# A trunk with mixture-of-experts layer, one core: heavy and light experts in turn instead of four heavy ones and then four light ones

## The chip, the cores and the metric

The program runs on one core of a Trainium2 chip. The metric is the device time of one execution in microseconds (us), 1356.88 us as the median of 3 runs of the kernel before (1356.76 to 1357.43).

The engines are TensorE (PE in the tables; PEld is its loading of the stationary operand), VectorE (DVE), ScalarE (ACT), GpSimd (POOL) and SyncE (SP), which here issues nearly all loads.

## The reference, cut to what matters

Two layers on 256 tokens of width 1024, all in float32. Each layer has a block of four token mixers and a feed-forward part. That of layer 0 is dense. That of layer 1, about half of the time, is a mixture of 8 experts of which each token takes two:

```
def swiglu(t, w1, w3, w2):
    return (jax.nn.silu(t @ w1) * (t @ w3)) @ w2

def moe_swiglu(h, router, w1, w3, w2):
    logits = (t @ router);  top_vals, top_idx = lax.top_k(logits, 2)
    weights = jax.nn.softmax(top_vals, axis=-1)
    combine = sum(one_hot(top_idx, 8) * weights)            # (256, 8)
    out = combine[:, 0:1] * swiglu(t, w1[0], w3[0], w2[0])
    for e in range(1, 8):
        out = out + combine[:, e:e+1] * swiglu(t, w1[e], w3[e], w2[e])
```

w1 and w3 of an expert are 1024 x 2816, w2 is 2816 x 1024; the three are 34.6 MB, those of eight experts 277 MB. A final RMSNorm follows.

## The kernel before

**Products in pieces.** A float32 weight tile is split into a part `hi` (ACT, a copy to fp32r, L145) and a rest `lo` (DVE, raw minus hi, L165); activations are split in the same way. A product is then `prod` (L579): hi by hi, activation lo by weight hi, activation hi by weight lo, three matmuls for each block of 128 rows.

**Tiles and homes.** All weights come in tiles of 128 x 2048 floats (1 MB, in transfers 1024.0 KB). `WeightStream` (L65) holds a plan, which is the list of all tiles in the order of their use. A tile is loaded by SP into a "raw" home, split into a "hi" home and a "lo" home, and multiplied. `SLOTS` (L40) names the homes of each phase of the program by letters; a letter can be raw in one phase and hi or lo in another. `take` picks a home whose last owner is done. A load can be issued when the lo split of the raw home's last owner is done, a hi split when PE is done with the hi home's last owner, and a lo split likewise. How many raw homes a phase has is so how far loads can run ahead of PE.

**An expert** has six chunks of columns, `CHUNKS`: five of 512 and one of 256. The program goes in steps (expert, chunk): the tiles of w1 and w3 of a step (two each, one each for the short chunk), then the w2 tiles of the step before (two, or one). An expert has 33 tiles' worth of weights.

**Heavy and light.** The experts are sorted on the chip by their number of tokens, expert 0 first whatever its number. SP reads the sorted order into registers (L1197) and loads the weights of an expert by register. The first four places (`e < LIGHT`) are heavy: 128 token slots, `prod` with three products, ACT's silu (L1231), DVE's product (L1232), four transposes on PE (L1357), split into `ah` and `al`. The last four are light: up to 64 tokens each, hi and lo of the tokens side by side as 128 columns, so `both` (L586) needs two products, one with the weight's hi and one with its lo. The two halves are then added by matmuls with a folded identity (L1440), and silu, product and splitting are done on 64 columns.

**Around them.** `gather` (L1246) picks the tokens of a group of experts from the normed tokens `th`, `tl` by matmuls with 0/1 matrices `picks`: group 0 is places 0 and 1, group 1 places 2 and 3, group 2 places 4 to 7. After each pair of places `scatter` adds their outputs to x: 16 matmuls (L1595) and four additions on DVE (L1604); places 6 and 7 are added singly. `place` and `weigh` make the matrix and the weights for that, once for each pair (5th step of the even place).

**Order.** In steps 1 to 23 (heavy) the order of the instructions is found by a scheduler at build time. From step 24 on, `light` writes it out by hand: with each tile `i` of the plan PE's matmuls come first, then ACT's hi split of tile i+4, then DVE's lo split of tile i+2 (`AHEAD_HI`, `AHEAD_LO`), with a list `todo` of what else goes on each engine behind which tile. Engines work in this order.

**Routing** is ahead of that, while PE multiplies the first chunk of expert 0 for all tokens (`dense`, banks `da` and `db`). DVE finds the two best experts of each token, casts the choice to bf16 (`selb`, L1057), and PE counts positions by matmuls with it (`posps`, L1061) between the `dense` matmuls.

Of the kernel before, what the change touches and what calls it, by code (L numbers as in the profile page):

```python
# [18 lines left out]
P = 128  # L19
D = 1024  # L20
# [24 lines left out]
    "moe0": {"raw": "ABCDHLstuwxyz", "hi": "EFG", "lo": "IJK"},  # L45
    "moe1": {"raw": "ABCDHLstux", "hi": "EFG", "lo": "IJK"},
    "moe2": {"raw": "ABCDHLstu", "hi": "EFG", "lo": "IJK"},
    "moe3": {"raw": "ABCDstu", "hi": "EFGH", "lo": "IJKL"},
    "moe4": {"raw": "ABCDstuyz", "hi": "EFGH", "lo": "IJKL"},
    "moe5": {"raw": "ABCDstyz", "hi": "EFGH", "lo": "IJKL"},  # L50
    "end": {"raw": "ABCDstyz", "hi": "EFGH", "lo": "IJKL"},
# [6 lines left out]
M0, M1, ML, MQ, M2, END = 6, 11, 24, 27, 40, 47  # L58
# [12 lines left out]
class WeightStream:  # L71
# [6 lines left out]
    def __init__(self, tc, plan, slots):  # L78
        self.tc, self.nc, self.plan, self.slots = tc, tc.nc, plan, slots
        self.gate = []  # L80
        self.pools, self.owner = {}, {}
# [8 lines left out]
    def open(self, pool, names):  # L90
        for name in names:
            self.pools[name] = pool

    def take(self, kind, j, dt):
# [13 lines left out]
        return self.pools[slot].tile([P, 2048], dt, tag=slot, name=slot)  # L108
# [123 lines left out]
class Trunk:  # L232
# [758 lines left out]
    def setup_moe(self, l):  # L991
# [14 lines left out]
        self.fold = self.const.tile([P, Q], F32, name="fold")  # L1006
# [83 lines left out]
    def rank(self, mp, rp, cnt, pos):  # L1090
# [10 lines left out]
        number = self.slots[:, :NE]  # L1101
        to = rp.tile(pairs, F32, name="to")
        nc.vector.tensor_tensor(
            to, rank[:, None, :].to_broadcast(pairs), number[:, :, None].to_broadcast(pairs), op=ALU.is_equal
# [59 lines left out]
    def moe(self, l, next_gain):  # L1164
# [5 lines left out]
        with self.pool("moe") as mp:  # L1170
            self.line_up(mp, 320)
# [39 lines left out]
            self.overflow(l, th, tl, cw, pos, cnti)  # L1211

    def picks(self, ep, pos, group):


        shape, e0 = ([P, 2, 1, P], 2 * group) if group < 2 else ([P, 4, 2, Q], LIGHT)
        n, size = shape[1], shape[3]
        out = []
        for t in range(NT):
            room = ep.tile([P, 2 * T], F32R, tag=f"pick{t}", name=f"pick{t}")  # L1220
            pick = room[:, : n * shape[2] * size].rearrange("p (e d s) -> p e d s", e=n, d=shape[2])
            self.nc.vector.tensor_tensor(
                pick, self.slots[:, None, None, :size].to_broadcast(shape),
                pos[:, t, e0 : e0 + n, None, None].to_broadcast(shape), op=ALU.is_equal,
# [15 lines left out]
    def experts(self, l, ep, ap, xp, tok, cw, pos, pick, g0):  # L1240
# [5 lines left out]
        def gather(group, part, bank=self.mm):  # L1246
            if part == 0:
                if group == 1:
                    xe[1] = tuple(self.extra.tile([P, NK, 2, P], F32R, tag=n, name="xe" + n) for n in "yz")
                else:  # L1250
                    room = xp.tile([P, 2 * 2048], F32R, tag="xe", name="xe")
                    if group == 0:
                        xe[0] = tuple(
                            room[:, j * 2048 : (j + 1) * 2048].rearrange("p (k e s) -> p k e s", k=NK, e=2) for j in range(2)
                        )
                    else:
                        x4 = room.rearrange("p (k e s) -> p k e s", k=NK, e=4)
                        xe[2] = x4[:, :, :, :Q], x4[:, :, :, Q:]
                        xe["both"] = x4
            ps = bank("gps")  # L1260
            d0 = 2 * part
            n = xe[group][0].shape[2]
            for d in range(2):
                self.pick_cols(
                    ps[:, d * T : (d + 1) * T].rearrange("p (e s) -> p e s", e=n), tok,
                    slice((d0 + d) * P, (d0 + d + 1) * P), pick,
                )
            self.hilo(*(x[:, d0 : d0 + 2] for x in xe[group]), ps.rearrange("p (d e s) -> p d e s", d=2, e=n))

        for part in range(4):  # L1270
            gather(0, part, self.acc)
# [3 lines left out]
        def first_act():  # L1275

            act = act_pair()
            for f0 in range(0, 4, 2):
                ps = self.mm("g0ps")
                for f in range(2):  # L1280
                    self.pick_cols(ps[:, f * T : (f + 1) * T].rearrange("p (e s) -> p e s", e=2), g0, slice((f0 + f) * P, (f0 + f + 1) * P), pick)
# [3 lines left out]
        steps = [(e, c) for e in range(NE) for c in range(len(CHUNKS))]  # L1285
        acts, ys, done = {0: first_act()}, {}, []
        wsl = ep.tile([P, NE], F32, name="wsl")

        def mask(t, pair, j):
            return pick[t][:, 2 * pair + j - (LIGHT if pair >= 2 else 2 * pair)].rearrange("p d s -> p (d s)")  # L1290
# [37 lines left out]
        for s in range(1, ML):  # L1328
# [3 lines left out]
            xv = xe[e // 2]  # L1332
            outs = []
            for nm in ("w1", "w3"):
                ps = self.mm(nm)
                nt = NK // nk
                for k0 in range(nt):
                    w = ws.get((nm, l, e, c, k0))
                    self.prod(
                        ps[:, :n], lambda i, k: xv[i][:, k0 * nk + k, e % 2, :], lambda j, k: w[j][:, k, :],  # L1340
# [4 lines left out]
            if len(done) == 2:  # L1345
                self.scatter(done, put)
                done = []
            if s % 12 == PLACE:
                put = place(s // 12)
                weigh(s // 12)  # L1350
            y = self.expert_down(l, ep, *steps[s - 1], acts.pop(s - 1), ys, wsl)
            if y is not None:
                done.append((steps[s - 1][0], y))
            nf = n // P
            ps = self.mm("actps")
            for f in range(nf):
                nc.tensor.transpose(ps[:, f * P : (f + 1) * P], g[:, f * P : (f + 1) * P], self.ident)  # L1357
            act = act_pair()
            self.hilo(*(x[:, :nf, :] for x in act), ps[:, :n].rearrange("p (f s) -> p f s", f=nf))
            acts[s] = act  # L1360
            if e in (1, 3) and c < 4:
                if c == 0:
                    pick = self.picks(ep, pos, e // 2 + 1)
                gather(e // 2 + 1, c)
# [11 lines left out]

        ws.release()
# [4 lines left out]
    def light(self, l, ep, ap, x4, acts, ys, done, wsl, masks, place_parts):  # L1382
# [3 lines left out]
        bank, half, now = {}, {}, [0]  # L1386
# [11 lines left out]
        def up(i, w, nm, e, c, k0):  # L1398
            c0, n = CHUNKS[c]
            nk, s = 2048 // n, e * len(CHUNKS) + c  # L1400
            if k0 == 0:
# [3 lines left out]
            self.both(  # L1405
                ps[:, :n], lambda k: x4[:, k0 * nk + k, e - LIGHT, :], lambda j, k: w[j][:, k, :],
                range(nk), start=k0 == 0, stop=last,
            )
            if nm == "w1" and k0 == 0:
                if s % 12 == PLACE:  # L1410
# [14 lines left out]

            def copy():
# [6 lines left out]
            nf, box = n // P, {}  # L1433
# [100 lines left out]
    def down_part(self, e, ps, act, k0, rhs, start, stop):  # L1534
        if e < LIGHT:
# [4 lines left out]
    def expert_down(self, l, ep, e, c, act, ys, wsl):  # L1540
# [4 lines left out]
        c0, n = CHUNKS[c]  # L1545
        for k0 in range(n // 256):
            w = ws.get(("w2", l, e, c, k0))
            for half in range(2):
                self.down_part(
                    e, y[half], act, k0, lambda j, k: w[j][:, k, half * 512 : (half + 1) * 512],  # L1550
                    c == 0 and k0 == 0, c == len(CHUNKS) - 1 and k0 == n // 256 - 1,
# [203 lines left out]
```

## Time and profile before

| | |
|---|---|
| device time, median of 3 | 1356.88 us |
| profiled execution, own time | 1354.36 us |
| its span | 1352.7 us |
| PE / PEld busy | 1308.0 / 1154.1 us |
| DVE / ACT / POOL busy | 1055.1 / 871.5 / 29.2 us |
| HBM read | 384.99 MB, 285 GB/s over the span |

The page's row of 40 slices shows DMA at 110 to 370 GB/s in the first three quarters and at 407 to 412 GB/s in the last quarter, without a break until the last slice. The mixture is in the second half: the first step of expert 0 begins at 595 us, place 1 at 709.4 us, place 4 (the first light one) at 1002 us, and the last matmuls are at 1339 us. A busy time of PE is a union of modelled, overlapping spans; a time between two instructions of one kind is the better measure of its pace.

### The profile page before, as it was taken

What the parts mean: (1) busy time and instruction counts of PE and PEld (TensorE: products, weight loads), DVE (VectorE), ACT (ScalarE), POOL (GpSimd) and SP (SyncE); (2) the same over time, 40 slices, a digit from 0 to 9 for tenths busy, and PEclk for the clock granted to TensorE, in tenths of its full rate; (3) what the DMA queues carried; (4) which work ended last, traced back from release to release, by engine and by line L of the source; (5) the groups of instructions that cost most, each with busy time, mean ns of one, the idle gap of its engine ahead of it and who ended that gap; (6) DMA issues with size and microseconds to landing.
All of it is one profiled execution on the core that took longest, in us unless ns stands there. A gap on an engine that the chain in (4) does not pass through costs nothing. (4 is left out here: it accounts for less than half of the span.)

```text
span 1352.7 us, 20123 instructions
## 1 busy us (share of the span) xinstructions
PE 1308.0 (97%) x8088; PEld 1154.1 (85%) x8088; DVE 1055.1 (78%) x874; ACT 871.5 (64%) x775; POOL 29.2 (2%) x52
## 2 busy tenths in 40 slices
PE   7999999999999999999999999999999989999995
PEld 7999999999989999978888888888887877777774
DVE  6976666444457856668988888988899989899996
ACT  5644445344437354556777777777788988888884
POOL 3110000000000000000000000000000000000000
PEclk9999999999999999999999999999999989999998
DMA  9736655555546395647989999999899999999992
GB/s 290 245 128 216 197 192 193 196 183 190 191 144 227 125 342 189 196 170 265 368 291 350 352 325 327 378 366 351 332 336 407 408 412 409 410 411 409 411 409 111
DMA packets 212128, 387.40 MB, mean 286 GB/s; under 512 B 7791, under 2 KB 98733, under 8 KB 212030
## 3 DMA queue, kind: packets, MB, share of 16 engines
q1 hardware_dynamic: 211214, 383.90, 78.6%
q0 software_dynamic: 816, 2.17, 0.6%
q8 instruction: 65, 1.06, 0.3%
q14 instruction: 33, 0.27, 0.0%
HBM read 384.99 MB, written 1.05 MB: 285 GB/s over the span
## 5 line engine op out<-in xcount | busy, mean ns | idle before, releaser
L165 DVE TENSOR_TENSOR J<-B,F 128x2048 fp32r<-128x2048 f32 (+1 forms) x33 | 72.2, 2189 | 36.6 <-ACT F L145 35.4
L145 ACT ACTIVATE F<-B 128x2048 fp32r<-128x2048 f32 (+1 forms) x33 | 60.6, 1838 | 41.0 <-PE mm L584 14.8
L165 DVE TENSOR_TENSOR L<-D,H 128x2048 fp32r<-128x2048 f32 (+1 forms) x29 | 64.1, 2213 | 24.3 <-ACT H L145 24.3
L165 DVE TENSOR_TENSOR I<-A,E 128x2048 fp32r<-128x2048 f32 (+1 forms) x27 | 59.7, 2210 | 27.2 <-ACT E L145 27.1
L871 ACT ACTIVATE sg<-mm,cols 128x256 f32<-128x256 f32 x64 | 26.8, 470 | 77.8 <-PE mm L584 49.7
L145 ACT ACTIVATE E<-A 128x2048 fp32r<-128x2048 f32 (+1 forms) x27 | 50.0, 1851 | 36.1 <-issue 12.6
L145 ACT ACTIVATE H<-D 128x2048 fp32r<-128x2048 f32 (+1 forms) x29 | 53.8, 1857 | 28.6 <-PE mm L584 11.0
L165 DVE TENSOR_TENSOR K<-C,G 128x2048 fp32r<-128x2048 f32 x24 | 55.0, 2290 | 16.8 <-ACT G L145 16.7
L145 ACT ACTIVATE G<-C 128x2048 fp32r<-128x2048 f32 x24 | 45.9, 1914 | 25.6 <-issue 11.7
L1440 PEld LDWEIGHTS actps<-fold,half 128*128 128x128 f32 x352 | 43.0, 191 | 2.2
L877 DVE TENSOR_TENSOR sg<-pr,sg 128x512 f32<-128x512 f32 x24 | 16.6, 692 | 33.2 <-ACT sg L871 33.2
L165 DVE TENSOR_TENSOR I<-s,E 128x2048 fp32r<-128x2048 f32 (+1 forms) x19 | 41.2, 2173 | 1.5 <-ACT E L145 1.3
L1440 PE MATMUL actps<-fold,half 128*128 128x64 f32 x352 | 41.9, 271 | 0.0
L145 ACT ACTIVATE E<-s 128x2048 fp32r<-128x2048 f32 (+1 forms) x19 | 34.6, 1827 | 9.3 <-PE w L584 5.5
L482 POOL TENSOR_TENSOR rstd<-rstd,mhalf 128x1 f32<-128x1 f32 (+1 forms) x14 | 12.5, 895 | 1284.1 <-ACT fo L487 744.0
L584 PE MATMUL w<-E,xe 128*128 128x512 f32 (+1 forms) x168 | 38.9, 372 | 0.0
L584 PE MATMUL mm<-hThi,F 128*128 128x256 f32 x256 | 35.9, 281 | 0.0
L584 PE MATMUL mm<-hThi,J 128*128 128x256 f32 x256 | 35.3, 279 | 0.0
L584 PE MATMUL mm<-hTlo,F 128*128 128x256 f32 x256 | 34.9, 278 | 0.0
L584 PE MATMUL mm<-hThi,G 128*128 128x256 f32 x240 | 33.8, 281 | 0.0
L584 PE MATMUL mm<-hTlo,G 128*128 128x256 f32 x240 | 33.6, 280 | 0.0
L584 PE MATMUL mm<-hThi,H 128*128 128x256 f32 x240 | 33.6, 280 | 0.0
(586 smaller groups left out, 3937.4 us busy)
## 6 DMA issues: line engine op xcount, KB each, us to landing
B<-in_moe_w_dram SPq DMA_DIRECT2D x29, 1024.0 KB, 5.6
C<-in_moe_w_dram SPq DMA_DIRECT2D x29, 1024.0 KB, 6.5
D<-in_moe_w_dram SPq DMA_DIRECT2D x29, 1024.0 KB, 9.5
s<-in_moe_w_dram SPq DMA_DIRECT2D x29, 1024.0 KB, 7.1
A<-in_moe_w_dram SPq DMA_DIRECT2D x28, 1024.0 KB, 10.8
t<-in_moe_w_dram SPq DMA_DIRECT2D x28, 1024.0 KB, 10.4
u<-in_moe_w_dram SPq DMA_DIRECT2D x24, 1024.0 KB, 8.1
y<-in_moe_w_dram SPq DMA_DIRECT2D x17, 1024.0 KB, 13.0
```

What stands on the lines that cost most here:

```text
L145: self.nc.scalar.activation(t[:, s], self.raw[j][:, s], AF.Copy)
L165: self.nc.vector.tensor_tensor(t[:, s], self.raw[j][:, s], self.hi[j][:, s].bitcast(F32), op=ALU.subtract)
L482: self.power = nc.gpsimd.tensor_tensor(r, t, self.mhalf[:, :n], op=ALU.pow)
L584: nc.tensor.matmul(ps, lhs(i, k), rhs(j, k), start=start and n == 0, stop=stop and n == len(steps) - 1)
L871: nc.scalar.activation(sg[:, s], psg[:, s], AF.Sigmoid, bias=self.col(l, "b_gate", i * 8 + 2 * j + c))
L877: nc.vector.tensor_tensor(sg, pr[j], sg, op=ALU.mult)
L1440: nc.tensor.matmul(out[:, o : o + Q], x[:, f * P : (f + 1) * P], self.fold, start=True, stop=True)
```

## The change

The order of the experts' places is now heavy, light, heavy, light, and so on: `RANK_AT` says which rank stands at which place. Groups to be gathered are places 0 and 2, "light" (1, 3, 5, 7), and places 4 and 6. Only the six steps of place 0 are left to the scheduler, and the seven other places are written out by hand in `rest`, which has got a branch for heavy places. The light tokens are gathered in steps 2 to 5 of place 0 (they were in place 3), the second heavy group in steps 18 to 21, in place 3. Picks have two sets of tiles.

The homes: the hi homes of the mixture are EFGH throughout (EFG for steps 1 to 23 before), the lo homes IJK throughout (IJKL from step 24 before). Raw homes are 12, 10, 9, 8, 10, 9, 9 in the phases that begin at steps 1, 2, 6, 11, 24, 40 and 47 (13 from step 1, 10 from 6, 9 from 11, 7 from 24, 9 from 27, 8 from 40 before). From step 24 on the tiles of `th` and `tl` are two of these homes (p and q, in rooms of 2048 + 128 floats). So that they can be reused, POOL writes the two tiles of normed tokens to DRAM (512.0 KB each) just after routing, for a branch (`overflow`) that runs only when an expert has more tokens than slots.

```
-    "moe0": {"raw": "ABCDHLstuwxyz", "hi": "EFG", "lo": "IJK"},
...
-    "moe3": {"raw": "ABCDstu", "hi": "EFGH", "lo": "IJKL"},
-    "moe4": {"raw": "ABCDstuyz", "hi": "EFGH", "lo": "IJKL"},
...
+    "moe0": {"raw": "ABCDLstuwxyz", "hi": "EFGH", "lo": "IJK"},
...
+    "moe3": {"raw": "ABCDLstu", "hi": "EFGH", "lo": "IJK"},
+    "moe4": {"raw": "ABCDLstupq", "hi": "EFGH", "lo": "IJK"},
...
-PHASES = ((1, "late"), (M0, "moe0"), (M1, "moe1"), (ML, "moe2"), (MQ, "moe3"), (M2, "moe4"), (END, "moe5"), (99, "end"))
+PHASES = ((1, "late"), (2, "moe0"), (6, "moe1"), (11, "moe2"), (24, "moe3"), (M2, "moe4"), (47, "moe5"), (99, "end"))
+RANK_AT = (0, 4, 1, 5, 2, 6, 3, 7)
+GATHER = 18
...
+                        for t in range(NT):
+                            nc.gpsimd.dma_start(self.a["normed"][t], self.htok[t])
...
+        ws.open(self.ypool, "pq", [(n, 2048 + 128) for n in ("yhi", "ylo")])
         ws.release()
         with self.tc.manual_schedule(engines={ACT, DVE, PE}):
-            self.light(l, ep, ap, xe["both"], acts, ys, done, wsl, masks, place_parts)
+            self.rest(l, ep, ap, xe, acts, act_pair, ys, wsl, masks, place_parts, gather_parts)
...
+            light = e % 2 == 1
+            if light:
+                x = xe["light"][e // 4]
+                self.both(
...
+            else:
+                x = xe[e // 4]
+                self.prod(
...
+            if not light:
+                if nm == "w1":
...
+                    at("hi", i + 4, silu)
+                    return
...
+                at("lo", i + 3, mult)
+                at("mm", i + 2, turn)
+                at("hi", i + 6, act_hi)
+                at("lo", i + 5, act_lo)
+                return
...
-        if e < LIGHT:
+        if e % 2 == 0:
             self.prod(ps, lambda i, k: act[i][:, 2 * k0 + k, :], rhs, range(2), start=start, stop=stop)
```

Of the instructions' order two places matter. The first is on PE, where a heavy and a light expert meet. Before, there is one such place, where step 23 ends and step 24 begins (`w` are the sums of w1 and w3, `yps` those of w2, `xe` the gathered tokens, E to H hi homes and I to L lo homes):

```order
L584 MATMUL yps<-I,ah 128x512 x4
L1357 MATMUL actps<-ident,g 128x128 x2
L590 MATMUL w_9497<-H,xe 128x512 x4
L590 MATMUL w_9497<-L,xe 128x512 x4
L590 MATMUL w_9497<-F,xe 128x512 x4
L590 MATMUL w_9497<-J,xe 128x512 x4
L590 MATMUL w_9524<-G,xe 128x512 x4
L590 MATMUL w_9524<-K,xe 128x512 x4
L590 MATMUL w_9524<-E,xe 128x512 x4
L590 MATMUL w_9524<-I,xe 128x512 x4
```

Now such places stand at every sixth step; this one is from light place 1 to heavy place 2:

```order
L594 MATMUL yps<-I,act 128x512 x2
L1527 MATMUL actps<-fold,half 128x64 x4
L588 MATMUL w_7915<-E,xe 128x512 x8
L588 MATMUL w_7915<-J,xe 128x512 x4
L588 MATMUL w_7915<-F,xe 128x512 x8
L588 MATMUL w_7915<-K,xe 128x512 x4
L588 MATMUL w_7957<-G,xe 128x512 x8
L588 MATMUL w_7957<-I,xe 128x512 x4
L588 MATMUL w_7957<-H,xe 128x512 x8
L588 MATMUL w_7957<-J,xe 128x512 x4
```

A tile takes eight matmuls in a light expert and twelve in a heavy one; the change alternates stretches of 33 tiles of the two kinds.

The second place is on DVE, in the routing ahead of the experts. Before (`selb` is what PE's position matmuls wait for; I, J are lo homes, y, z raw ones):

```order
L1025 TENSOR_REDUCE top_k<-top_m 128x2
L1026 TENSOR_TENSOR top_m<-top_m,top_k 128x16
L1055 TENSOR_TENSOR sel<-top_m 128x16
L1057 CAST selb<-sel 128x16
L165 TENSOR_TENSOR I<-y,E 128x2048
L1067 SCALAR_TENSOR_TENSOR pos<-posps,sel 128x16
L1070 TENSOR_SCALAR pos<-pos 128x16
L1096 SCALAR_TENSOR_TENSOR key<-posps,first_key 128x8
L165 TENSOR_TENSOR J<-z,F 128x2048
```

And now:

```order
L1032 TENSOR_REDUCE top_k<-top_m 128x2
L169 TENSOR_TENSOR I<-y,H 128x2048
L1033 TENSOR_TENSOR top_m<-top_m,top_k 128x16
L1062 TENSOR_TENSOR sel<-top_m 128x16
L169 TENSOR_TENSOR J<-z,E 128x2048
L1064 CAST selb<-sel 128x16
L1074 SCALAR_TENSOR_TENSOR pos<-posps,sel 128x16
```

Two lo splits have moved ahead of the cast. On PE nothing has moved there: the position matmuls still stand behind the `db<-J` matmuls of the second token tile and ahead of the `db<-G` ones.

## Rows read from the trace of the kernel before

**Rows 1.** Windows: busy us (instructions) of PE, PEld, DVE, ACT, POOL; clock; DMA; GB/s.

```profile
1002.00:1082.35 80.35, 78.30 (x398) 64.28 (x397) 77.73 (x51) 71.87 (x60) 0.00 (x0) 1.00 1.04 409
1082.35:1167.10 84.75, 77.79 (x370) 62.59 (x369) 79.21 (x48) 72.16 (x60) 0.00 (x0) 0.94 1.05 410
1167.10:1250.70 83.60, 78.89 (x394) 63.27 (x393) 79.30 (x53) 71.83 (x61) 0.00 (x0) 1.00 1.05 410
1250.70:1337.40 86.70, 80.61 (x388) 62.49 (x387) 80.71 (x62) 70.71 (x69) 0.00 (x0) 1.00 0.90 353
709.40:1002.00 292.60, 292.60 (x1417) 244.93 (x1416) 258.97 (x158) 215.66 (x152) 0.00 (x0) 1.00 0.94 344
```

**Rows 2.** Timeline of PE, light steps: start, us, what; a fold ends a step.

```profile
1057.27 1.89 PE L1440 MATMUL actps<-fold,half 128*128 128x64 f32 x16
1071.14 1.89 PE L1440 MATMUL actps<-fold,half 128*128 128x64 f32 x16
...
1081.35 1.00 PE L1440 MATMUL actps<-fold,half 128*128 128x64 f32 x8
...
1166.11 1.00 PE L1440 MATMUL actps<-fold,half 128*128 128x64 f32 x8
...
1249.68 1.00 PE L1440 MATMUL actps<-fold,half 128*128 128x64 f32 x8
...
1323.00 1.90 PE L1440 MATMUL actps<-fold,half 128*128 128x64 f32 x16
...
1337.41 2.45 PE L1578 MATMUL scps<-y,put 128*128 128x512 f32 x8
```

**Rows 3.** Timeline of DVE, inside a light step.

```profile
1128.25 2.28 DVE L165 TENSOR_TENSOR L<-D,H 128x2048 fp32r<-128x2048 f32 x1
1130.45 0.42 DVE L1457 TENSOR_TENSOR act<-gf,act 128x256 fp32r<-128x256 f32 x1
1130.79 2.28 DVE L165 TENSOR_TENSOR J<-y,F 128x2048 fp32r<-128x2048 f32 x1
```

**Rows 4.** Timeline of PE, heavy steps; the transposes end a step.

```profile
840.91 0.60 PE L1357 MATMUL actps<-ident,g 128*128 128x128 f32 x4
...
858.91 0.60 PE L1357 MATMUL actps<-ident,g 128*128 128x128 f32 x4
875.85 0.60 PE L1357 MATMUL actps<-ident,g 128*128 128x128 f32 x4
...
936.35 0.60 PE L1357 MATMUL actps<-ident,g 128*128 128x128 f32 x4
954.20 0.60 PE L1357 MATMUL actps<-ident,g 128*128 128x128 f32 x4
```

**Rows 5.** DVE's groups in place 4: the additions of a scatter.

```profile
L1604 DVE TENSOR_TENSOR x<-x,scps 128x512 f32<-128x512 f32 x4 | 2.6, 678 | 0.0
```

**Rows 6.** Timeline of PE in the routing.

```profile
613.84 1.08 PE L584 MATMUL da<-I,hThi 128*128 128x512 f32 x4
...
616.58 1.08 PE L584 MATMUL db<-J,hThi 128*128 128x512 f32 x4
617.51 0.18 PE L1061 MATMUL posps<-selb,before 128*128 128x8 bf16 x1
```

**Rows 7.** Timeline of DVE in the routing.

```profile
614.49 0.18 DVE L1055 TENSOR_TENSOR sel<-top_m 128x16 f32<-128x16 f32 x1
614.70 0.17 DVE L1057 CAST selb<-sel 128x16 bf16<-128x16 f32 x1
```

**Rows 8.** Timeline of ACT in the routing.

```profile
622.57 1.92 ACT L145 ACTIVATE G<-C 128x2048 fp32r<-128x2048 f32 x1 [3.82 <-DVE sort L1110]
```

**Rows 9.** DMA issues: queue, times, size, us from issue to landing.

```profile
gain<-in_norm_ffn_dram POOLq DMA_DIRECT2D x2, 512.0 KB, 6.4
B<-in_moe_w_dram SPq DMA_DIRECT2D x29, 1024.0 KB, 5.6
```

**Rows 10.** Waits in places 4 to 7: total, times, longest.

```profile
PE yps L590 <- DVE act L1457: 3.6, 2, 2.0
```

More of the change, by code (lines that the diff above doesn't have):

```diff
@@ L107, in take @@
         self.owner[slot] = (kind, j)
[L108 removed]
+        tag, size = self.tags[slot]
+        return self.pools[slot].tile([P, size], dt, tag=tag, name=slot)[:, :2048]
     def pair_due(self, slot, j):
@@ L1210, in moe @@
                     self.experts(l, ep, ap, xp, (th, tl), scw, spos, pick, (gh, gl))
-            self.overflow(l, th, tl, cw, pos, cnti)
+            self.overflow(l, cw, pos, cnti)
     def picks(self, ep, pos, group):
-        shape, e0 = ([P, 2, 1, P], 2 * group) if group < 2 else ([P, 4, 2, Q], LIGHT)
+        if group == "light":
+            shape, part = [P, 4, 2, Q], slice(1, NE, 2)
+        else:
+            shape, part = [P, 2, 1, P], slice(4 * group, 4 * group + 3, 2)
         n, size = shape[1], shape[3]
@@ L1244, in experts, with room, gather_sums @@
         xe = {}
[L1246 to L1259, printed above, removed]
+        def room(group):
+            if group == "light":
+                xe[group] = [self.extra.tile([P, NK, 2, P], F32R, tag=n, name="xe" + n) for n in "yz"]
+            else:
+                x = xp.tile([P, 2 * 2048], F32R, tag="xe", name="xe")
+                xe[group] = tuple(
+                    x[:, j * 2048 : (j + 1) * 2048].rearrange("p (k e s) -> p k e s", k=NK, e=2) for j in range(2)
+                )
+        def gather_sums(group, part, bank):
             ps = bank("gps")
-            d0 = 2 * part
-            n = xe[group][0].shape[2]
+            n = 4 if group == "light" else 2
             for d in range(2):
@@ L1326, in set_weights @@
             )
-        for s in range(1, ML):
+        for s in range(1, len(CHUNKS)):
             e, c = steps[s]
@@ L1344, in experts @@
             g = self.gate(ep, *outs, n)
[L1345 to L1364, printed above, removed]
+            if s == PLACE:
+                put = place(0)
+                weigh(0)
+            self.expert_down(l, *steps[s - 1], acts.pop(s - 1), ys)
+            acts[s] = self.turned(act_pair(), g, n // P)
+            if s >= 2:
+                if s == 2:
+                    room("light")
+                gather("light", s - 2)
         masks = {"put": put}
@@ L1375, in place_parts, with gather_parts, turned, turn @@
             )
+        def gather_parts(group, part):
+            box = {}
+            if part == 0:
+                pick[group] = self.picks(ep, pos, group)
+                room(group)
+            return (
+                lambda: box.update(ps=gather_sums(group, part, self.mm)),
+                lambda: gather_hi(group, part, box["ps"]), lambda: gather_lo(group, part, box["ps"]),
+            )
+        ws.open(self.ypool, "pq", [(n, 2048 + 128) for n in ("yhi", "ylo")])
         ws.release()
         with self.tc.manual_schedule(engines={ACT, DVE, PE}):
-            self.light(l, ep, ap, xe["both"], acts, ys, done, wsl, masks, place_parts)
+            self.rest(l, ep, ap, xe, acts, act_pair, ys, wsl, masks, place_parts, gather_parts)
         self.last_down(l, acts, ys[NE - 1], wsl, masks["put"])
-    def light(self, l, ep, ap, x4, acts, ys, done, wsl, masks, place_parts):
+    def turned(self, act, g, nf):
+        ps = self.turn(g, nf)
+        self.hilo(*(x[:, :nf, :] for x in act), ps[:, : nf * P].rearrange("p (f s) -> p f s", f=nf))
+        return act
+    def turn(self, g, nf):
+        ps = self.mm("actps")
+        for f in range(nf):
+            self.nc.tensor.transpose(ps[:, f * P : (f + 1) * P], g[:, f * P : (f + 1) * P], self.ident)
+        return ps
+    def rest(self, l, ep, ap, xe, acts, act_pair, ys, wsl, masks, place_parts, gather_parts):
         nc, ws = self.nc, self.ws
         todo = {"mm": [], "hi": [], "lo": []}
-        bank, half, now = {}, {}, [0]
+        bank, half, done = {}, {}, []
         def at(kind, j, f):
@@ L1544, in expert_down @@
         y = ys[e]
-        c0, n = CHUNKS[c]
-        for k0 in range(n // 256):
+        for k0 in range(CHUNKS[c][1] // 256):
             w = ws.get(("w2", l, e, c, k0))
@@ L1581, in last_down @@
                     nc.vector.tensor_tensor(self.x[t][:, s], self.x[t][:, s], ps, op=ALU.add)
-    def scatter(self, done, put):
-        for t in range(NT):
-            self.add_scattered(t, self.scatter_half(done, put, t))
     def scatter_half(self, done, put, t):
@@ L1613, in overflow @@
                 hf = op.tile([P, NT, D], F32, name="hf")
-                nc.vector.tensor_tensor(hf, th.bitcast(F32), tl.bitcast(F32), op=ALU.add)
+                for t in range(NT):
+                    nc.sync.dma_start(hf[:, t, :], self.a["normed"][t])
                 slots = op.tile([P, P], F32, name="slots2")
```

113 lines of the change are left out of this document (75 added, 38 removed).

## Prediction

> **What bounds the kernel now.** I first read busy times by window, one window for each light place and one for the three heavy places that the change puts among them, then the timelines of PE and DVE inside them. In the heavy window PE has no gap (292.60 of 292.60 us) and DMA moves 344 GB/s; in places 4 to 6 DMA moves 409 to 410 GB/s at a share of 1.04 to 1.05 and PE has gaps [rows 1]. The reader is to see that the two kinds of place have different limits.
>
> Heavy: a plain step takes 858.91 to 875.85, 16.94 us [rows 4], so six tiles at 2.82 us each, and a place of 5.5 steps 93.2 us. A tile of 1.049 MB takes 2.56 us at 410 GB/s: DMA could bring 36 tiles in that time, and the place takes 33. It is PE's stage, and DMA is held back for want of free homes.
>
> Light: 33 tiles at 2.56 us are 84.4 us, and places 5 and 6 took 84.75 and 83.6 [rows 1, 2]. Those are DMA's. Place 4 took 80.35: it began with loads already landed. What sets its pace is DVE. The starts on DVE give 2.20 us for a lo split and 0.34 for a small operation [rows 3]; a step has six of the one and two of the other, 13.88 us, and PE's folds at 1057.27 and 1071.14 are 13.87 us apart [rows 2]. DVE was busy 77.73 of the 80.35 us [rows 1].
>
> So the loads are late at the end and idle before it, and a place with landed loads runs at DVE's pace, not much under DMA's. That bounds what evening out the loads can give: some 7 us for each light place that now waits for DMA.
>
> **The change part by part.**
>
> *Four light places behind heavy ones.* Each now begins as place 4 did, with PE and DVE coming out of a heavy place. Place 4 holds four additions of a scatter, 2.6 us [rows 5]; these now fall into the next heavy place, where PE is the limit. That leaves 80.35 - 2.6 = 77.75 us. Place 3 gets the gathering of the second heavy group: four lo operations as long as an addition, 0.68 us [rows 5], and two picks of half the columns, 0.34 each by estimate: 3.4 us on DVE. Place 7 keeps the additions of place 6 (2.6) and its longer end: from the last fold of a full step 14.4 us (1323.00 to 1337.41), against 11.2 in place 4 (1071.14 to 1082.35) [rows 2], so 3.2. Sum: 4 x 77.75 + 3.4 + 2.6 + 3.2 = 320.2 us. Before, the four took 1002.0 to 1337.4, 335.4 us. **-15.2 us.**
>
> *Three heavy places between them* (2, 4, 6). PE's work counts: 93.2 us each, a scatter of 16 matmuls at 16.94 / 72 = 0.235 us, 3.8 us, and the masks of a pair, 18.00 - 16.94 = 1.06 us (840.91 to 858.91 against the plain step) [rows 4]. Three times 98.1 us is 294.3; places 1 to 3 took 292.6 with one scatter, one set of masks and two gatherings. **+1.7 us.**
>
> *The light gathering in place 0.* A step with a gathering takes 17.85 us (936.35 to 954.20), 0.91 more than a plain one [rows 4], and place 0 is heavy: four of them. **+3.6 us.**
>
> *Routing.* The order on DVE now has two lo splits ahead of the cast to `selb`. The first needs home I, in use until 613.84 + 1.08 = 614.9 [rows 6]: it ends at 617.1, the two small operations behind it, 0.2 each [rows 7], at 617.5. The second needs home J, in use until 616.58 + 1.08 = 617.7 [rows 6]: it ends at 619.9, and the cast at 620.1. It ended at 614.9 before [rows 7]. PE comes to the position matmuls at 617.5 [rows 6], so it waits 2.6 us, and the `db` matmuls, the first gathering and what else PE has queued wait behind it. A hi split of 1.92 us, which ACT did from 622.57 on [rows 8], has its like now ahead of the splitting of `g`; most of that is hidden by the gathering that PE does meanwhile, and I add 0.4. **+3.0 us**, with bounds of 0 (should DVE find the homes free early) and 6 (both in full and the small waits of the tables).
>
> *What I cost at nothing.* The two writes of normed tokens: POOL is idle there, such transfers landed 6.4 us after issue [rows 9], and the room of those tiles is written again only when PE's `dense` matmuls are over, some 6 us behind the position matmuls; their 1.05 MB are 2.6 us of DMA at a time when the loads wait for homes. Uncovered it is up to 6.4 us. Homes p and q add stock, which is worth 0 where stock suffices. Three lo homes in place of four in the light places: the split of tile i+2 then waits for PE's end of tile i-1, which is past whenever DVE is the late one. The heavy places in an order by hand: no trace shows that. In the light places, which have it, PE waited 3.6 us in 22 steps for activations [rows 10], 0.16 a step; for 16.5 heavy steps that makes 2.7 us at the most that a row supports, and a gain is excluded since PE had no gap there. I take 0, as the slack in a heavy step is larger.
>
> *What the -15.2 rests on.* In 77.75 us DMA brings 30.4 tiles, so 2.6 of the 33 must have landed when a light place begins. In 98.1 us of a heavy place DMA can bring 38.3 and 33 are used, so a refill of 5.3 is to be had. There are 8 raw homes at the tightest (steps 11 to 23). A load takes 5.6 us from issue to landing where it need not queue [rows 9], 2.2 homes, and one is being split; nearly five remain. For a pair of places DMA needs 66 x 2.56 = 169 us, and PE and DVE 98.1 + 77.75 = 175.9. It fits, with 4% to spare.
>
> The rate in that is the measured one, 409 to 410 GB/s over 248 us [rows 1]. The Trainium skill ("DMA: Bandwidth & Descriptors", Specifications) gives a core about 358 GB/s as its share of HBM. By that a place of 34.6 MB would take 96.7 us, and seven of them 677 us in place of 614.5, for a time of about 1412 us. The trace disagrees, and the measurement decides.
>
> **Sum.** -15.2 + 1.7 + 3.6 + 3.0 = -6.9 us on the profiled execution of 1354.36 us, so 1347.5; the median lies 2.5 above that execution, so **1350.0 us** for the median.
>
> **The rivals.**
>
> *Light places at PE's pace.* If PE's own work were the limit: its loading was busy 64.28 us in place 4, and in the heavy window, where PE is full, 244.93 of 292.60, 0.837 [rows 1]. 64.28 / 0.837 = 76.8, less the scatter's 3.8 makes 73.0 us, 4.75 under my 77.75; four times that gives 1331. The Trainium skill ("Trainium Kernel Development and Optimization", Best Practices) asks to judge the distance to the limit by the busy share of the weight loading and not of the matmuls. The trace agrees: PE's matmul row reads 78.30 of 80.35 where the loading leaves more room. For it: at each crossing from heavy to light DVE is ahead by up to two splits, and now there are four crossings. Against it: place 4 had that too, and two splits are all the lead that the order allows. Chance 0.10.
>
> *Loads do not carry over (slower).* If the stock at the start of a light place is nil, DMA's pace stays: 84.75 us for each of three and 86.7 for the last, 341.0 in place of 320.2: 1370.8 us. Each missing tile costs 2.56 us; the forecast gain is gone when 0.7 tiles are missing in each of the four, that is with a stock below 1.9. For it: one home fewer than before in steps 11 to 23, and a pair of places leaves only 4%. Against it: the heavy window's 344 GB/s shows a DMA that waits for homes, so the homes are full there. Chance 0.14.
>
> *The heavy order by hand stalls PE.* If a transpose came late by 1 us in each of 16.5 steps: 1366.5 us. Against it: the transpose stands two tiles (5.6 us) behind the sums, and DVE has only a split (2.2 us) and the product ahead of it. Chance 0.05.
>
> *It does what it says and the parts cancel*: half of the stock and the upper bound in routing give 1350.0 + 0.35 x 20.8 = 1357. Chance 0.13.
>
> **Numbers.** The forecast has 0.58, with a range of its own of 1343 to 1354. The measurement can tell about 0.2% (2.7 us) from no change. Faster by more: 0.58 + 0.10 = 0.68; within: 0.13; slower: 0.14 + 0.05 = 0.19. The range for 8 in 10 reaches half-way to the first rival and two thirds of the way to the second: 1336 to 1365.
>
> **What the profile after would show.** Right: PE without gaps in heavy places of about 98 us; light places of 77 to 81 us, in which DVE is busy over 95% and DMA no longer the last to come; DMA at 380 to 410 GB/s in both kinds; and in the routing a gap of PE of about 2.6 us ahead of the position matmuls. Wrong: waits of ACT's hi splits for DMA in the second half of light places (the second rival), PE waiting for `g` in heavy ones (the third), or light steps well under 13.9 us (the first).

## The result and the profile after

The changed kernel takes 1342.51 us (median of 4 runs, 1341.23 to 1342.77) against 1356.82 us, a ratio of 0.9893 (0.9879 to 0.9908): 14.3 us faster, where 6.9 was forecast. The direction was right, and so was the mechanism in the light places; the size was half of what came.

The profiled execution took 1342.27 us, with a span of 1340.5. One window for each place from 1 to 7, the columns as in rows 1:

```profile
716.70:795.10 78.40, 74.95 (x382) 61.25 (x381) 76.77 (x48) 72.35 (x61) 0.00 (x0) 1.00 1.03 395
795.10:891.40 96.30, 96.30 (x463) 80.76 (x463) 87.17 (x56) 69.60 (x50) 0.00 (x0) 1.00 1.03 393
891.40:971.60 80.20, 76.97 (x406) 64.36 (x405) 78.83 (x52) 73.48 (x63) 0.00 (x0) 1.00 1.02 387
971.60:1068.00 96.40, 96.40 (x464) 80.86 (x463) 87.01 (x55) 69.90 (x50) 0.00 (x0) 1.00 1.05 410
1068.00:1145.50 77.50, 73.97 (x374) 60.30 (x373) 76.10 (x46) 71.68 (x59) 0.00 (x0) 1.00 1.04 403
1145.50:1241.90 96.40, 96.40 (x463) 80.85 (x463) 87.14 (x56) 69.69 (x50) 0.00 (x0) 1.00 1.03 393
1241.90:1326.70 84.80, 81.96 (x400) 64.81 (x399) 80.95 (x61) 70.78 (x69) 0.00 (x0) 1.00 0.81 300
```

In the heavy places (second, fourth and sixth row) PE has no gap and DMA moves 393 to 410 GB/s, against 344 before [rows 1]. In the light ones DVE is busy for 98% (76.77 of 78.40, 76.10 of 77.50), and DMA is under its 410. That is what the prediction said would be seen; only the last place, which has the longer end and in which the loads run out, is outside it (84.80 us, 300 GB/s).

For lengths I take one mark for every place, the start of its last folds or transposes, since a window's edge can lie anywhere between two places. A place lasts from the mark of the place ahead of it to its own. Before: 709.16, 807.21, 904.55, 1001.66, 1081.35, 1166.11, 1249.68 and 1337.41 (last scatter). After: 716.35, 794.05, 891.10, 970.61, 1067.66, 1144.48, 1241.53 and 1324.64. These are from PE's timeline; of after, with the first step's transposes ahead:

```profile
651.41 0.60 PE L1421 MATMUL actps<-ident,g 128*128 128x128 f32 x4
...
716.35 0.38 PE L1421 MATMUL actps<-ident,g 128*128 128x128 f32 x2
...
844.88 0.60 PE L1421 MATMUL actps<-ident,g 128*128 128x128 f32 x4
861.70 0.60 PE L1421 MATMUL actps<-ident,g 128*128 128x128 f32 x4
...
891.10 0.38 PE L1421 MATMUL actps<-ident,g 128*128 128x128 f32 x2
...
1106.99 1.89 PE L1527 MATMUL actps<-fold,half 128*128 128x64 f32 x16
1120.87 1.89 PE L1527 MATMUL actps<-fold,half 128*128 128x64 f32 x16
...
1324.64 2.46 PE L1656 MATMUL scps<-y,put 128*128 128x512 f32 x8
```

| us on the marks | before | after | difference | forecast |
|---|---|---|---|---|
| four light places and the end | 335.75 | 317.14 | -18.6 | -15.2 |
| three heavy places | 292.50 | 291.15 | -1.35 | +1.7 |
| place 0 behind its first step | 62.61 | 64.94 | +2.3 | +3.6 |
| routing to the first step's transposes | 646.55 | 651.41, of it 1.15 from the first 40 us | +3.7 | +3.0 |
| sum | | | -13.9 | -6.9 |

The 1.15 us do not belong to the change. In the first 40 us PE waits for the first loads and small tiles, and from there the offset changes by 0.2 us at the most until the routing (by up to 0.6 in the runs below): one and the same matmul of before and of after, in the first 40 us,

```profile
31.68 1.13 PE L584 MATMUL psg<-hThi,glr_hi 128*16 128x256 f32 x8 [0.70 <-ACT glr_hi L470]
```

```profile
32.98 1.10 PE L588 MATMUL psg<-hThi,glr_hi 128*16 128x256 f32 x8 [1.33 <-ACT glr_hi L474]
```

stands 1.30 us apart, and one at 437.55 us before starts at 438.69 after. In the runs below this head, the stretch ahead of the routing, is 0.6 to 4.7 us longer than in the profiled execution of before, for programs that have the same instructions there. So I compare places, and take a difference of medians under 2 us for unclear.

A light step is 1120.87 - 1106.99 = 13.88 us, the 13.88 of the prediction. A plain heavy step is 861.70 - 844.88 = 16.82 us; before it was 16.94 [rows 4]. In the routing:

```profile
621.36 0.18 PE L1068 MATMUL posps<-selb,before 128*128 128x8 bf16 x1 [2.53 <-DVE selb L1064]
```

and on DVE ahead of it:

```profile
616.18 2.29 DVE L169 TENSOR_TENSOR I<-y,H 128x2048 fp32r<-128x2048 f32 x1 [0.77 <-PE da L588]
...
618.93 2.29 DVE L169 TENSOR_TENSOR J<-z,E 128x2048 fp32r<-128x2048 f32 x1 [0.16 <-PE db L588]
621.14 0.17 DVE L1064 CAST selb<-sel 128x16 bf16<-128x16 f32 x1
```

Each of the two splits waits for PE to be done with its home, and PE waits 2.53 us for the cast behind them (forecast 2.6).

Not all of the +3.7 is that wait. In this execution the granted clock of PE was at 0.50, the lower of its two levels (1.2 in place of 2.4 GHz), from 622.9 to 626.3 us, a little behind the wait. The first line is from there; the second is the same group in another execution of the same kernel ("the changed kernel again", below), which had the same wait of 2.53 us and whose clock stayed up:

```profile
622.51 1.56 PE L588 MATMUL db<-G,hTlo 128*128 128x512 f32 x4
```

```profile
623.59 1.08 PE L588 MATMUL db<-G,hTlo 128*128 128x512 f32 x4
```

From the position matmuls to the gathering PE takes 7.32 us in the first and 5.72 in the second, and with the heads taken out the second reaches the first step's transposes 1.4 us earlier: its routing costs +2.3. Of the nine traces of this case that have the wait, three show the low clock behind it; of the five without the wait, none does.

### The profile page after: what moved, and what is told of

It reads as the page before. It is cut to its first block, busy times and chain, and to the rows that moved or that the text cites. A ratio compares the mean times of both kernels' runs of the same rounds, so it can differ in the third digit from the quotient of the medians.

```text
span 1340.5 us, 20363 instructions
## 1 busy us (share of the span) xinstructions
PE 1297.7 (97%) x8088; PEld 1151.5 (86%) x8088; DVE 1055.1 (79%) x878; ACT 869.4 (65%) x779; POOL 30.8 (2%) x62
## 5 line engine op out<-in xcount | busy, mean ns | idle before, releaser
L149 ACT ACTIVATE F<-B 128x2048 fp32r<-128x2048 f32 x37 | 70.9, 1915 | 46.5 <-PE mm L588 14.8
L169 DVE TENSOR_TENSOR J<-B,F 128x2048 fp32r<-128x2048 f32 x25 | 57.3, 2291 | 36.3 <-ACT F L149 34.4
L169 DVE TENSOR_TENSOR L<-D,H 128x2048 fp32r<-128x2048 f32 x20 | 45.8, 2290 | 24.3 <-ACT H L149 24.3
L169 DVE TENSOR_TENSOR K<-C,G 128x2048 fp32r<-128x2048 f32 x21 | 48.1, 2290 | 16.4 <-ACT G L149 16.3
L149 ACT ACTIVATE H<-D 128x2048 fp32r<-128x2048 f32 x22 | 42.2, 1917 | 25.4 <-PE mm L588 11.0
L149 ACT ACTIVATE G<-C 128x2048 fp32r<-128x2048 f32 x22 | 42.1, 1914 | 22.7 <-issue 11.7
L588 PE MATMUL w<-F,xe 128*128 128x512 f32 (+1 forms) x184 | 43.0, 375 | 0.0
L588 PE MATMUL w<-H,xe 128*128 128x512 f32 (+1 forms) x184 | 42.9, 374 | 0.0
L588 PE MATMUL w<-G,xe 128*128 128x512 f32 (+1 forms) x184 | 42.0, 372 | 0.0
L588 PE MATMUL w<-I,xe 128*128 128x512 f32 (+1 forms) x172 | 42.0, 370 | 0.0
L588 PEld LDWEIGHTS w<-G,xe 128*128 128x128 f32 x184 | 32.3, 189 | 5.8
L588 PEld LDWEIGHTS w<-E,xe 128*128 128x128 f32 x184 | 32.3, 189 | 5.8
```

The costliest lines, as they stand in the source:

```text
L149: self.nc.scalar.activation(t[:, s], self.raw[j][:, s], AF.Copy)
L169: self.nc.vector.tensor_tensor(t[:, s], self.raw[j][:, s], self.hi[j][:, s].bitcast(F32), op=ALU.subtract)
L588: nc.tensor.matmul(ps, lhs(i, k), rhs(j, k), start=start and n == 0, stop=stop and n == len(steps) - 1)
```

## The experiments

### Where the heavy step's 0.13 us come from

The matmuls of w1 and w3 take the same time in both kernels; only those of w2 differ. In one view of the tile `yps` on PE (durations in ns: shortest, median, longest), before:

```profile
L584 PE MATMUL yps<-F,ah x8: 390/395/404, 852.4 to 871.4; 128*128 128x512 f32 x8
L584 PE MATMUL yps<-F,al x8: 392/392/404, 852.9 to 871.9; 128*128 128x512 f32 x8
```

and after:

```profile
L588 PE MATMUL yps<-E,ah x8: 389/389/389, 842.2 to 877.4; 128*128 128x512 f32 x8
L588 PE MATMUL yps<-E,al x8: 389/389/389, 842.6 to 877.8; 128*128 128x512 f32 x8
```

Two tiles of w2 in a step, 2.80 us each before and 2.73 after, are the 0.13 to 0.14. Place 0, which the scheduler still orders, has it too (668.22 - 651.41 = 16.81), so the order by hand is not the cause. Two things remain: the fourth hi home, and addresses. The diff sets a pad from 320 to 192 bytes, widens `fold` and gives the picks a second set of tiles, and in the built programs `ah` lies at byte 191872 of a partition before (a multiple of 512 plus 384) and at 194048 after (a multiple of 512). Moving only the pad, in either kernel, tells them apart.

```
-            self.line_up(mp, 320)
+            self.line_up(mp, 448)      # in the kernel before: ah at 192000, a multiple of 512
```

> The kernel before with one number changed: the pad ahead of the mixture's tiles is 448 bytes in place of 320, so that everything in that pool, the activations ah and al among it, lies 128 bytes further. Theory (addresses): the w2 products take 0.07 us less for each heavy tile because ah and al then start at a multiple of 512 bytes; a plain heavy step goes from 16.94 to 16.80 us, and with 22 steps the time falls by about 3 us, to 1354 from 1357. Rival (four hi homes in place of three, or the order by hand, made the heavy steps faster): the step stays at 16.94 us and the time at 1357.

Measured: 1354.08 us, ratio 0.9974 (0.9963 to 0.9984), 3.2 us faster; steps of 16.79 to 16.81 us:

```profile
858.57 0.60 PE L1357 MATMUL actps<-ident,g 128*128 128x128 f32 x4
875.36 0.60 PE L1357 MATMUL actps<-ident,g 128*128 128x128 f32 x4
```

```
-            self.line_up(mp, 192)
+            self.line_up(mp, 320)      # in the changed kernel: ah at 194176, a multiple of 512 plus 128
```

> The changed kernel with the same pad larger by 128 bytes (320 in place of 192). Theory (addresses): plain heavy steps go from 16.81 back to 16.94 us, in all 22 of them some 3 us: 1345.5 against 1342.5. Rival (four hi homes or the order by hand): the step stays at 16.81 us and the time at 1342.5.

Measured: 1346.58 us, ratio to before 0.9925 (0.9909 to 0.9941), some 4 us slower than the changed kernel; plain steps of 16.93 to 16.95 us, and the matmuls:

```profile
L588 PE MATMUL yps<-E,ah x8: 390/392/396, 842.4 to 877.9; 128*128 128x512 f32 x8
L588 PE MATMUL yps<-E,al x8: 395/400/404, 842.8 to 878.3; 128*128 128x512 f32 x8
```

So it is the address of the activations, with three hi homes and with four: 22 heavy steps at 0.14 us are 3.1 us. In the profiled execution of the first of the two, the slowest of its eight, the heavy steps are 2.9 us shorter together and the light places 1.7 us longer; the median shows the whole 3.2.

### How much is due to the turns

```
-RANK_AT = (0, 4, 1, 5, 2, 6, 3, 7)
+RANK_AT = (0, 1, 2, 3, 4, 5, 6, 7)
...
-            light = e % 2 == 1
+            light = e >= LIGHT
```

(and the groups, rooms and gathering steps that go with it, as before the change.)

> The changed kernel with the four heavy places first and the four light ones behind them, as before; order by hand, homes, addresses, routing and the writes to DRAM stay as changed. Groups are gathered in place 1 (second heavy group) and place 3 (light). Theory (evening out the loads is what pays): the light places go back to the pace of DMA, 80 to 85 us each and 335 us for the four, 18 more than in turn; against that place 0 is 3 us shorter, since no gathering stands there, with as much in places 1 and 3: 1357 us, near the kernel before. Rival (order by hand, addresses and more homes are what pays): 1343 to 1347.

Measured: 1353.67 us, ratio 0.9973 (0.9964 to 0.9983). That is 11 us more than the changed kernel and 3 less than the one before. The turns carry the 11 us. The 3 are a balance, on the marks and without the head: the heavy places and place 0 are 2.2 us shorter (moving the pad alone made them 2.9 shorter), the light places 3.5 shorter, and the routing, with its wait, 2.0 longer. The expected 1357 was 3 us too high: I had the light places back at DMA's pace but for the first, and the second stayed short too, at 78.6 us; only the third fell to that pace:

```profile
1002.50:1082.70 80.20, 77.92 (x397) 64.03 (x396) 78.87 (x51) 72.25 (x60) 0.00 (x0) 1.00 1.04 400
1082.70:1161.30 78.60, 73.44 (x369) 59.51 (x369) 77.38 (x48) 70.58 (x60) 0.00 (x0) 1.00 1.04 411
1161.30:1245.80 84.50, 79.14 (x393) 62.90 (x393) 80.93 (x53) 72.84 (x61) 0.00 (x0) 1.00 1.04 410
```

Before, the second was at 84.75 [rows 1]; here 10 raw homes stand in steps 24 to 39, where before there were 7 and then 9. That the homes are the reason was not tested by itself.

### Whether PE's wait in the routing counts

```
+            with ExitStack() as gate:                 # in lo_parts, around the split
+                if self.behind:
+                    gate.enter_context(self.tc.issue_after(self.behind.pop(0).ins))
```

(`behind` holds the casts to selb and to the order, and the key.)

> The changed kernel in which the three lo splits of the routing stay behind the cast to selb, the key and the order on DVE, as they stood before. Theory (the wait of PE for selb is on the path): the 2.53 us wait ahead of the position matmuls is gone, and PE reaches the first transposes of place 0 3 to 3.7 us earlier; time 1339 us. Rival (what comes behind, the first gathering or late loads, takes the gain back): 1342.5 us, with a new wait of PE or of the loads in the first step of place 0.

Measured: 1341.74 us, ratio 0.988 (0.9865 to 0.9896), by the medians 0.8 us less, which is unclear. In the trace the wait for `selb` is gone, and against its head, 4.7 us longer than that of before, PE reaches the position matmuls 2.66 us earlier. But a new wait of 1.57 us for weights stands in the step:

```profile
622.25 0.18 PE L1072 MATMUL posps<-selb,before 128*128 128x8 bf16 x1
...
647.62 0.35 PE L1354 MATMUL wslps<-cw,pick 128*128 128x2 f32 x2 [1.57 <-DVE cw L479]
...
652.70 0.60 PE L1427 MATMUL actps<-ident,g 128*128 128x128 f32 x4
```

The first transposes come 2.26 us earlier than in the profiled execution of the changed kernel, the last scatter 2.35; but some 1.4 of that is the low clock which that execution had in its routing. Against the execution whose clock stayed up there, the first transposes come 0.8 us earlier and the last scatter 0.9, as much as the medians. So the wait is on the path, and most of what its removal gives is taken back behind it, 1.57 us by the new wait: the rival's mechanism, for all but 0.8 us. Of the head, one part is that the granted clock was at 0.50 from 35.3 to 38.7 us here; what else lengthened it I did not find.

### Stock: the homes p and q, and how many raw homes are needed

```
-    "moe4": {"raw": "ABCDLstupq", ...        -    "moe5": {"raw": "ABCDLstpq", ...
+    "moe4": {"raw": "ABCDLstu", ...          +    "moe5": {"raw": "ABCDLst", ...
```

> The changed kernel without the two padded homes: p and q are taken off the lists, so that 8 raw homes stand in steps 24 to 39 and 7 from step 40 on, in place of 10 and 9. The writes of the normed tokens stay. Theory (a light place needs 2.6 landed tiles at its start, and 7 or 8 homes hold more than that): light places stay within 1 us of 77 us, the time stays at 1342.5 within 1.5. Rival (every home is one more tile of stock that the light place uses, 2.56 us each): places 5 and 7 lose up to 5 us each, 1347 to 1352.

Measured: 1343.59 us, ratio 0.9897 (0.9881 to 0.9914), 1.1 more than the changed kernel and inside what I call unclear. Places 3 and 5 are as long as before this edit (79.47 and 76.85 us on the marks, against 79.51 and 76.82); place 7 with its end, on 7 homes, takes 87.4 in place of 83.1 (84.7 in the run without the writes, further down, which has the same homes; in the 87.4 the granted clock was at 0.50 for 3.4 us near the end). So 8 homes suffice for places 3 and 5, and p and q serve the last place alone.

```
-    "moe3": {"raw": "ABCDLstu", ...
+    "moe3": {"raw": "ABCDst", ...            # and so in moe4, moe5 and end; moe2 "ABCDLstu"
```

> The changed kernel with 6 raw homes from step 11 on (8, 10, 9 and 9 before that edit) and 8 in steps 6 to 10. Theory (stock is homes less 2.2 in flight and one being split, so 2.8 of the 2.6 tiles needed): at the edge, light places 3, 5 and 7 0 to 2 us longer, 1342 to 1348. Rival (each home less costs a tile of 2.56 us in each of three light places): 15 to 25 us slower, 1358 to 1368, with PE's or ACT's waits for loads in the second half of each light place.

Measured: 1357.17 us, ratio 1.0004 (0.9994 to 1.0014): the whole gain is gone. Place 3 takes 86.87 us on the marks, place 5 81.89, place 7 with its end 87.4; the heavy places stay at 97.05. The theory had 1342 to 1348, the rival 1358 to 1368: the rival's size nearly came, not the theory's. In place 3 one step takes 17.24 us (932.78 to 950.02), where ACT waits for loads:

```profile
932.78 1.89 PE L1527 MATMUL actps<-fold,half 128*128 128x64 f32 x16
950.02 1.89 PE L1527 MATMUL actps<-fold,half 128*128 128x64 f32 x16
```

```profile
ACT G L149 <- DMA D<-in_moe_w_dram: 2.6, 2, 1.9
```

In the heavy place ahead of it DMA moves 382 GB/s with 6 homes, 393 with 8. My count of the stock (homes less 2.2 in flight and one being split) left out the homes that a tile holds between its hi split, four tiles ahead of PE, and its lo split, two tiles ahead. With these two taken off as well, 8 homes leave 2.8 tiles and 6 leave 0.8, where 2.6 are needed; that fits both runs, but no run tests this count by itself.

### Whether DVE sets the light step

```
-                nc.vector.tensor_tensor(
+                nc.gpsimd.tensor_tensor(
                     act[:, :nf, Q:], box["g"]...
```

> The changed kernel with one of the two small operations of a light step, the lo part of the activations (128x256), on GpSimd in place of VectorE. Theory (a light step runs at VectorE's pace): steps fall from 13.88 to 13.54 us, with 20 such steps 6 to 7 us less, 1336. Rival 1 (DMA is as near a limit as VectorE): 0 to 2 us less, and new waits for loads. Rival 2 (GpSimd's operation slows the others down or comes too late for TensorE): 1343 or more.

Measured: 1373.82 us, ratio 1.009 (1.0053 to 1.0127): 31 us slower than the changed kernel. The step went from 13.88 to 14.10 us, and DVE shows why:

```profile
746.32 2.27 DVE L169 TENSOR_TENSOR K<-D,E 128x2048 fp32r<-128x2048 f32 x1
748.52 2.83 DVE L169 TENSOR_TENSOR I<-s,F 128x2048 fp32r<-128x2048 f32 x1
```

```profile
748.42 0.78 POOL L1544 TENSOR_TENSOR act<-gf,act 128x256 fp32r<-128x256 f32 x1 [11.12 <-ACT act L1540]
```

The split that runs beside GpSimd's operation takes 2.83 us in place of 2.28. DVE saves 0.34 us a step and loses 0.55, and the step is longer by just that difference: DVE sets it. By the Trainium skill ("SBUF — State Buffer", Who interferes with whom) a VectorE instruction with two inputs in SBUF contends with a GpSimd instruction that reads SBUF; the trace agrees. The larger part of the loss is elsewhere: PE waited for GpSimd's operation five times, 22.7 us in all. In places 1, 3 and 5 this falls into the short chunk's step, 16.4 us in place of 9.7 in the first: GpSimd's operation took 4.86 us beside three splits back to back, and PE waited 4.64 us for it. In place 7 it took 10.29 us beside five splits, and PE waited 5.99. A part of the longer steps is the clock: in each of these four places the granted clock went to 0.50 for 6.8 us from within the wait on (793.8 to 800.6 in place 1), and the pairs of matmuls behind it came 0.85 us apart in place of 0.46.

### A split more of lead

The changed kernel again, as a level for the next runs:

> The changed kernel unaltered, once more, beside the three below: the level that they are compared with, 1342.5 within 1.

Measured: 1341.76 us, ratio 0.9888 (0.9873 to 0.9904).

```
-    "moe4": {"raw": "ABCDLstupq", "hi": "EFGH", "lo": "IJK"},
+    "moe4": {"raw": "ABCDstupq", "hi": "EFGH", "lo": "IJKL"},     # and so in moe5 and end
...
             ws.ahead(0, i + 1 + AHEAD_LO)
+            if ws.plan[i][-1] in ("moe4", "moe5", "end"):
+                ws.split_lo()
```

> The changed kernel in which from step 24 on L is a lo home again (9 raw homes in steps 24 to 39 and 8 from step 40, in place of 10 and 9), and VectorE splits three tiles ahead of TensorE instead of two. Theory (a light place is as long as VectorE's work less the lead with which it comes out of the heavy place): one split of 2.2 us less in each of places 5 and 7, 1338. Rival 1 (DMA is as near): the homes less cost as much, 1341 to 1344. Rival 2 (TensorE's own work is nearly as long, so the lead is not used): 1342.

Measured: 1345.34 us, ratio 0.9913 (0.99 to 0.9927), not faster. In place 5 the gain comes and goes back. The second light step takes 11.33 us in place of 13.44, and at the end of the place PE waits 2.21 us for the short chunk's activations, which now stand behind one split more on DVE:

```profile
1078.65 1.89 PE L1527 MATMUL actps<-fold,half 128*128 128x64 f32 x16
1089.98 1.89 PE L1527 MATMUL actps<-fold,half 128*128 128x64 f32 x16
...
1139.49 0.73 PE L594 MATMUL yps<-G,act 128*128 128x512 f32 x2 [2.21 <-DVE act L1544]
```

The same with the order of the routing:

> Both edits together: the fourth lo home with a lead of three, and the casts of the routing ahead of the lo splits. Theory (both gains stand in different places and add): 2.3 us under the run with the fourth lo home alone, 1336. Rival (TensorE's wait in the routing is given back later): no difference between the two.

Measured: 1342.65 us, ratio 0.9898 (0.9881 to 0.9915), 2.7 less than without it. The traces place 0.7 of that in the routing, about as much as the order gave by itself: the first transposes come 0.7 us earlier against the head. The rest has no place in them, since the profiled execution without the order (1341.73) lay 3.6 under its median.

Then the fourth lo home and the routing's order, without the longer lead in DVE's order:

> The changed kernel with the casts of the routing ahead of the lo splits and with L as fourth lo home from step 24 on, but VectorE's order as in the changed kernel (two tiles ahead), so that a short chunk's activations do not stand behind one split more. Theory (the home alone lets VectorE come out of a heavy place with one split more, and the loss at the end of the light place came from the order): places 5 and 7 2 us shorter each, the routing 2.3 us, 1335.5 to 1338. Rival 1 (without the order the home gives no lead): the routing's 2.3 us alone, 1339.5. Rival 2 (the lead is lost in any case before the place ends, or the raw home less costs it): 1340 to 1343.

Measured: 1342.06 us, ratio 0.9892 (0.9875 to 0.991). Places 5 and 7 are 76.86 and 83.13 us on the marks, those of the changed kernel 76.82 and 83.11: the home alone gives no lead, as the first rival had it. The 2.3 us that the rival counted for the routing did not come: the first transposes are 0.8 us earlier, as in the run with that order alone. No version was found that is clearly faster than the changed kernel.

### Whether the writes to DRAM cost anything

The changed kernel without p and q and without the two writes; the branch for overfull experts adds `th` and `tl` again.

> The changed kernel without the two padded homes and without the two writes of the normed tokens to DRAM (the branch for overfull experts adds th and tl again, as before). Theory (the writes are hidden): the same as without the padded homes alone, 1343.6 within 1. Rival (they hold up the first loads of the mixture or the first gathering): up to 6 us less, 1338 to 1341.

Measured: 1345.58 us, ratio 0.9918 (0.9901 to 0.9935), 2 us more than with the writes, which is at the edge of what the head explains (2.2 us here, 0.9 there). From the first step's transposes to the end of place 6 both take 590.1 us, and with the heads taken out both reach these transposes within 0.2 us of each other. The writes cost nothing that shows.

## Why the prediction was right in direction and half in size

Two steps of the prediction failed. The sum gave each light place 77.75 us, and it takes 76.8; and it excluded any gain in the heavy places because PE had no gap, where the heavy steps became 0.13 us shorter each.

- **Light places, -15.2 forecast, -18.6 measured.** The mechanism is right: DVE's pace of 13.88 us in each, and loads that carry over. The misjudged term is the price of a place. Place 5, which holds neither a gathering nor the end, took 76.82 us, 0.93 less than the sum has, and four times that is 3.7. Of the 0.93, 0.66 come from taking place 4 as 80.35 us from a window whose edges I had chosen; on the marks it is 79.69. Smaller terms of either sign nearly cancel: the gathering in place 3 took 2.7 in place of 3.4 (79.51 less 76.82), the four places before are 0.35 longer on the marks, place 7 took 0.5 more than the sum gave it over the others, and the fourth gathering of place 0 fell behind the mark into place 1 (77.70, 0.9 more than place 5).
- **Heavy places, +1.7 forecast, -1.35 measured.** The step that failed is the sentence that a gain is excluded because PE had no gap. PE without gaps is not PE at its best pace: the same matmuls can take less time each. Addresses gave 0.14 us a step, 16.5 x 0.14 = 2.3 here and some 0.5 in place 0; moving the pad alone shows it in both kernels. I had read the pad in the diff as mere bookkeeping and had given it no term. The remaining 0.7 are left over by subtraction: a heavy place has 4.65 us beside its 5.5 plain steps (97.05 less 5.5 x 16.80) where masks and scatter had been put at 4.9, and rounding.
- **Gathering in place 0, +3.6 forecast, +2.3 measured.** A gathering costs 0.9 us as forecast (17.70 against 16.81); the fourth came behind the mark, in place 1, and some 0.5 are the addresses again.
- **Routing, +3.0 forecast, +3.7 measured, +2.3 where the clock stayed up.** The wait is 2.53 us, as forecast; the 0.4 added for ACT's hi split did not show. The 1.4 above it are the low clock of one execution, for which the sum had no term.
- **Costed at nothing.** The writes, the order by hand and three lo homes: right, as far as the runs can tell. The stock: the conclusion (8 homes suffice) was right, the count behind it wrong, as the run on 6 homes shows.
- **From the profile to the median.** I added 2.5 us because before's profiled execution lay so far under its median. After's lay 0.2 under. Such an offset belongs to one execution, whose head was the shortest of all that were profiled, so it should not have been carried over as a constant; how much of the 2.5 us is the head no run shows. The spans differ by 12.2 us, the medians by 14.3, the places by 13.9 (15.3 with the routing of the execution whose clock stayed up).

Of the rivals, the one with loads that do not carry over is the one that the run on 6 homes made nearly true; here the homes were enough. The first, light places at PE's pace, did not come: DVE stayed the limit.

## What to carry to other kernels

Where two kinds of stage have different limits, put them in turn only if the buffers can carry enough from the one to the other: here 8 homes kept the gain in places 3 and 5, and 6 lost all of it. A busy engine without gaps can still get faster, so look at the duration of one instruction in both programs, and at every change of an address. Measure stages by one kind of mark, take the start of the program out before comparing spans, and look at the granted clock of a stretch before putting its length down to the change.

## What the runs showed of the hardware

- In the lines shown, matmuls of 128x512 on the heavy activations took 390 to 404 ns where these start at a multiple of 512 bytes plus 128 or 384, and 389 at a multiple of 512; a heavy step took 16.93 to 16.95 us and 16.79 to 16.82. The gathered tokens, which before lay at a multiple of 512 plus 0 or plus 256, showed no such difference (389 ns at the median for both).
- A VectorE subtraction of 128x2048 from SBUF took 2.28 us alone and 2.83 in the step shown beside a GpSimd operation of 0.78 us. The same GpSimd operation took 4.86 us beside three such subtractions back to back and 10.29 beside five, and those took 2.28 to 2.29.
- The granted clock of PE went to 0.50 for 3.4 us behind a wait of 2.53 us in three of nine traces, and for 6.8 us from within waits of 4.6 to 6.0 us on in the run with GpSimd; groups of matmuls then took up to 1.91 us in place of 1.08.
- The first 40 us, in which all programs here have the same instructions, brought differences of up to 4.7 us between profiled executions, 1.0 us between two of the same program.
